# A transformer block on one core: attention scores issued two units ahead, values in pairs, FFN tiles in pools of their own, reloaded operands stored split

## The chip, the cores and the metric

One core of a Trainium2 chip runs one program. The metric is the device time of one execution in microseconds (us). The engines are TensorE (PE, with its weight load PEld), VectorE (DVE), ScalarE (ACT), GpSimd (POOL) and SyncE (SP), which only issues DMAs. Each engine takes its instructions in the order of the program and waits on semaphores; DMAs run on 16 shared DMA engines. PSUM is TensorE's output memory, SBUF the memory of all engines.

## The reference

```
h = modulate(rmsnorm(x), mod0, mod1);  z = h @ w_in        # x: 2048 tokens x 1024
att = neighbourhood_attention(q, k, v, k_ctx, v_ctx, rpb)  # 8 heads of 64, 8x16 query blocks
    s = concat(q.k_loc / 8 + bias, q.k_ctx / 8);  p = softmax(s);  out = p @ concat(v_loc, v_ctx)
y = concat(att, spatial_gating(z), conformer_conv(z)) @ w_out
x = x + mod2 * y
h2 = modulate(rmsnorm(x), mod3, mod4)
gate, up = split(h2 @ w_up)                                # 1024 -> 2 x 2816
x = x + mod5 * ((silu(dwconv(gate)) * up) @ w_down)        # a 3-wide convolution over tokens
return rmsnorm(x)
```

## The kernel before

Everything is fp32. A fp32 operand of a matmul is split into a high and a low part (`hh`, `hl`; for weights the two halves of a `...hl` tile): ACT copies the high part, DVE or POOL subtracts it from the source to get the low one (`halves`, `split_comb`; L1086 and L1087 for weights and for `ah`, L1116 and L1117 for the operands of the FFN). A product of two such operands is three matmuls of 128x512 (high by high, low by high, high by low).

**Attention (318 to 970 us in the trace).** 128 units, each one head of one block of 128 queries: (band, pr, cb, j), where `cb` is one of 4 column blocks and `j` one of a pair of heads. A unit is `scores` (TensorE into the one PSUM bank `s`, then DVE L684 adds the bias into `sb` and takes the maximum `mx`, a small DVE instruction negates it, ACT L689 takes the exponential), `turned` (TensorE transposes `sb` into the PSUM tile `tp`, ACT L719 and DVE L721 copy it to `pt`), and once for each pair of units `values` (TensorE multiplies `pt` by `vt` and `vcx` into `obank`). The order on TensorE is written out: scores(u+1), values(u-2) when `j` is 0, filler, turned(u), filler. The filler is the rest of the projections and of out_proj, pieces of generators; a piece ends at a `yield` with its price.

**The FFN** is a Strassen-Winograd scheme of 7 products over 2x2 blocks, named B11, T2, T1, T3, B21, T4, B22 and numbered 0 to 6 in tile names. Tokens are done in two halves, t = 0 and 1. For t = 0 `first_half` (beside the last piece of out_proj) and `first_half_rest` make the 7 operands in SBUF (`hh{p}_0`, `hl{p}_0`). For t = 1 `second_half` makes them while the up products of t = 0 run, and stores them unsplit to DRAM (`td[p]`); `reload` brings each back as four tiles `tc{p}{kk}` and splits them when the tiles of t = 0 come free. The up products (`g_..`, `u_..`, k = 0 to 10) run from 1062 to 1961 us, with weights staged by `up_weights` (sums on POOL, splits on ACT and DVE). Their results go to DRAM as `actd[t][p]`, one 256 KB store per k and product, issued by POOL.

**The last column.** The convolution needs one token from the other half, so `last_column` makes `pc` at the end of t = 1 and ACT issues five DMAs of single columns into `actd[0]` of T2, T1, T3, T4 and B22.

**The down products (1961 to 2430 us)** load `actd` back as `ra{t}{p}{k}` (two k at a time), split it to `ah`, combine and split weights `wd` to `dw{t}{p}{k}hl` and multiply; `add` adds a product from PSUM to the residual `x1r` (DVE L1450). All these loads go through SyncE's queue in the order of the code. `ahead` is a list of loads to be issued two at a time behind each `ra` load.

SBUF is laid out in pools that open and close in the order of a stack. A tile of a new pool waits for the last users of whatever lay at its address.

## Time and profile before

| | |
|---|---|
| median of 3 runs | 2447.9 us (2447.46 to 2448.69) |
| the profiled execution | 2451.56 us, span 2449.8 us |
| mean granted TensorE clock | 0.972 of full speed |
| PE busy | 2298.1 us, 94% of the span |
| DVE, ACT, POOL busy | 76%, 47%, 44% |
| DMA | 413.35 MB, 169 GB/s over the span |

The profiled execution lies 3.7 us above the median. A busy share is a mean over stages with different limits: TensorE is nearly full in most of them, and idles in a few short stretches, where the granted clock falls too. The time is to be read stage by stage.

### The profile page before, as it was taken

The numbers are of one execution on the slowest core, as the hardware profiler recorded it, in microseconds if no ns is written. First come the engines' busy times: TensorE is split into PE (matmuls) and PEld (weight loads), VectorE is DVE, ScalarE is ACT, GpSimd is POOL, SyncE is SP. The second block draws the span as 40 slices with busy tenths as digits, with TensorE's granted clock in tenths as the row PEclk, the third lists the DMA queues.
The fourth block names the chain that finished last, engine by engine and source line by source line (L and its number), as shares of the span: only waits on it lengthen the run. The fifth ranks groups of instructions, "written<-read, shape, count | busy, mean of one in ns | idle before, by whom it ended". The sixth has DMA issues, their size and how long they took to land.

```text
span 2449.8 us, 34599 instructions
## 1 busy us (share of the span) xinstructions
PE 2298.1 (94%) x12452; PEld 1905.2 (78%) x12452; DVE 1851.2 (76%) x2623; ACT 1146.4 (47%) x2020; POOL 1068.2 (44%) x990
## 2 busy tenths in 40 slices
PE   7999989999999999979999999899999979989996
PEld 5889768988877888858877787588888857868875
DVE  4785665556774974697888878787777769999997
ACT  5764643356455446454443434443443434444442
POOL 0265313011011221355656565366565457565743
PEclk9999999999999999989999999999999989999998
DMA  9675676558768788643334443533233492345322
GB/s 356 224 252 172 209 220 190 173 153 257 222 204 267 215 222 259 216 132 102 130 116 149 137 153 110 169 102 108 94 112 104 126 332 85 94 131 192 95 86 82
DMA packets 183403, 413.35 MB, mean 169 GB/s; under 512 B 27200, under 2 KB 76224, under 8 KB 181184
## 3 DMA queue, kind: packets, MB, share of 16 engines
q1 hardware_dynamic: 142768, 314.63, 41.3%
q0 software_dynamic: 27296, 90.20, 10.0%
q10 hardware_dynamic: 13168, 6.32, 1.0%
q8 instruction: 98, 1.61, 0.3%
q14 instruction: 73, 0.60, 0.1%
HBM read 307.49 MB, written 103.58 MB: 168 GB/s over the span
## 4 chain that ended last, share of the span: by engine, by line
PE 52%; DVE 21%; DMA 12%; issue 7%; POOL 4%; ACT 3%; SPq 1%; DVEq 0%; ACTq 0%; POOLq 0%
PE po L194 4%; DVE cv L565 3%; PE pk L194 3%; PE obank L194 3%; PE pv L1439 2%; PE pq L194 2%; PE tp L200 2%; DMA adaf<-in_ada 2%; PE s L194 2%; PE tp L194 2%; DMA kk<-ks 2%; DVE ah L1087 1%; PE pu L1439 1%; DMA xb<-x1d 1%; POOL ah L1087 1%
## 5 line engine op out<-in xcount | busy, mean ns | idle before, releaser
L565 DVE SCALAR_TENSOR_TENSOR cv<-hconv,cst,cv 128x512 f32<-128x512 f32 x240 | 213.6, 930 | 1.6 <-ACT cv L559 1.4
L684 DVE CUSTOM_DVE_ANT_0 sb<-s,bias_t 128x544 f32<-128x544 f32 (+3 forms) x128 | 105.1, 821 | 107.4 <-PE s L194 95.0
L689 ACT ACTIVATE sb<-sb,mx 128x544 f32<-128x544 f32 (+3 forms) x128 | 106.3, 831 | 156.9 <-DVE mx L687 143.0
L1296 DVE SCALAR_TENSOR_TENSOR c<-gb,cst,c 128x512 f32<-128x512 f32 x176 | 173.6, 1010 | 4.3 <-ACT c L1294 4.2
L1086 ACT ACTIVATE ah<-ra 128x512 fp32r<-128x512 f32 x154 | 94.6, 623 | 114.7 <-PE pu L1439 34.1
L1087 POOL TENSOR_TENSOR ah<-ra,ah 128x512 fp32r<-128x512 f32 x62 | 92.7, 1514 | 76.9 <-ACT ah L1086 76.9
L194 PE MATMUL s<-kk,qq 128*128 128x256 f32 (+4 forms) x512 | 103.0, 323 | 16.0 <-DMA kk<-ks 13.3
L194 PEld LDWEIGHTS s<-kk,qq 128*128 128x128 f32 x512 | 89.6, 193 | 35.3 <-issue 19.4
L200 PE MATMUL tp<-cst,sb 128*128 128x128 f32 (+2 forms) x672 | 98.2, 279 | 12.3 <-ACT sb L689 5.7
L200 PEld LDWEIGHTS tp<-cst,sb 128*128 128x128 f32 (+2 forms) x672 | 78.9, 140 | 25.6 <-ACT sb L689 6.1
L1087 DVE TENSOR_TENSOR ah<-ra,ah 128x512 fp32r<-128x512 f32 x92 | 90.1, 983 | 3.8 <-ACT ah L1086 3.8
L719 ACT ACTIVATE pt<-tp 128x384 f32<-128x384 f32 (+2 forms) x128 | 61.7, 482 | 50.5 <-PE tp L200 50.5
L188 POOL DMA_DIRECT2D x1d<-x x30 | 16.5, 551 | 146.2 <-DVE x L852 137.1
L1294 ACT ACTIVATE c<-gb,cst 128x512 f32<-128x512 f32 x88 | 69.1, 809 | 23.7 <-DVE gb L1269 22.5
L955 POOL TENSOR_TENSOR adaf<-adaf,adaf 128x1024 f32<-128x1024 f32 x16 | 41.8, 2615 | 87.9 <-ACT adaf L952 87.8
L721 DVE COPY pt<-tp 128x256 f32<-128x256 f32 (+1 forms) x128 | 57.5, 450 | 29.9 <-PE tp L200 28.5
L1298 ACT ACTIVATE c<-c 128x512 f32<-128x512 f32 x88 | 55.2, 629 | 43.0 <-DVE c L1296 42.9
L952 ACT ACTIVATE adaf<-adaf,silu_c 128x256 f32<-128x256 f32 x128 | 54.5, 497 | 42.2 <-DMA adaf<-in_ada 42.0
L188 POOL DMA_DIRECT2D actd<-c x66 | 36.5, 554 | 75.5 <-DVE c L1306 58.6
L188 POOL DMA_DIRECT2D ks<-k x60 | 33.5, 561 | 74.9 <-ACT k L218 53.2
L194 PE MATMUL obank<-pt,vt 128*64 128x128 f32 (+2 forms) x832 | 62.5, 285 | 2.1 <-ACT pt L719 2.1
L1306 DVE TENSOR_TENSOR c<-c,u 128x512 f32<-128x512 f32 x66 | 59.6, 904 | 0.4
(2408 smaller groups left out, 7970.6 us busy)
## 6 DMA issues: line engine op xcount, KB each, us to landing
ra<-actd SPq DMA_DIRECT2D x70, 512.0 KB
wg<-in_w_up SPq DMA_DIRECT2D x44, 512.0 KB
wu<-in_w_up SPq DMA_DIRECT2D x44, 512.0 KB
actd<-tt POOLq DMA_DIRECT2D x88, 256.0 KB, 2.4
actd<-c POOLq DMA_DIRECT2D x66, 256.0 KB, 2.3
adaf<-in_ada SPq DMA_DIRECT2D x32, 512.0 KB
qq<-qs SPq DMA_DIRECT2D x64, 256.0 KB
adaf<-in_ada SPq DMA_DIRECT2D x8, 1024.0 KB
```

Source lines behind the costliest of these rows:

```text
L188: st_eng[0].dma_start(plain(dst), plain(src))
L194: x = nc.tensor.matmul(*args, **kw)
L200: x = nc.tensor.transpose(*args)
L565: nc.vector.scalar_tensor_tensor(acc[ct], hb[:, ct, k:k + TB], cvw[:, ct, k:k + 1], acc[ct], op0=ALU.mult, op1=ALU.add)
L684: nc.vector.tensor_tensor_reduce(out=sb[:, w], in0=s[:, w], in1=bt[:, w], scale=1.0, scalar=-3.0e38, op0=ALU.add, op1=ALU.max, accum_out=m ...
L689: nc.scalar.activation(sb[:, w], sb[:, w], AF.Exp, bias=mx[:, 1:2], accum_out=rs[:, cb, j:j + 1])
L719: nc.scalar.activation(dst, src, AF.Copy)
L1086: nc.scalar.activation(hl[:, 0, :], src, AF.Copy)
L1087: eng.tensor_tensor(hl[:, 1, :], src, hl[:, 0, :].bitcast(F32), op=ALU.subtract)
L1294: nc.scalar.activation(c, gb[:, i, o:o + TB], AF.Identity, scale=fcw[:, f, 0:1], bias=fcw[:, f, 3:4])
L1296: nc.vector.scalar_tensor_tensor(c, gb[:, i, o + d:o + d + TB], fcw[:, f, d:d + 1], c, op0=ALU.mult, op1=ALU.add)
L1439: nc.tensor.matmul(ps[i], w[:, ww, sl], ah[:, aa, :], start=start and k_ == 0 and m == 0, stop=(k_ == NP - 1 and m == 2), skip_group_check ...
```

## The change

1. Attention: `scores` is issued two units ahead instead of one, `values` does two blocks (`cb`, `cb`+1) at once, four units late instead of two; its result leaves PSUM in one ACT copy and one DVE multiply for both. The scores are negated in the pass that adds the bias, so the small DVE negation (one for each unit) is gone. `sb`, `pt`, `vt` and `mx` have more buffers, and the filler yields twice as often, at half the price.
2. Pools: the tiles of the FFN's seven operands lie in a pool each, so do the two `mix` buffers and `pair`; small tiles move to the const pool; GpSimd's area for DMA descriptors shrinks from the default, 16384 bytes, to 4096.
3. FFN start: the operand T3 is split within `first_half` instead of behind out_proj.
4. Second half: the operands T2, T1, T3 and T4 of t = 1 are split before they are stored (ACT for the high part, DVE for T2 and T1, POOL for T3 and T4), stored as high and low, and `reload` loads them straight into `hh` and `hl`, in two DMAs of 1 MB each.
5. Down: the first three `wd` loads are issued together, all other loads of `ahead` are kept behind the last `ra` load, `x1r` has one pool of 16, the `add` of B11's product is handed out two at a time instead of at once at k = 7, and the low part of B22's `ah` is made by POOL for odd k.

```
-            if x % 2 and x < KT - 1:
-                yield 1.37 * n / TB
+            if x < KT - 1:
+                yield 0.685 * n / TB
...
-        mx = cp.tile([P, 2], F32, tag="mx", name="mx" + nm, bufs=2)
+        sb = pool.tile([P, 768], F32, tag="sb", name="sb" + nm, bufs=3)
+        mx = cp.tile([P, 1], F32, tag="mx", name="mx" + nm, bufs=3)
...
-        x = nc.vector.tensor_scalar(mx[:, 1:2], mx[:, 0:1], -1.0, None, op0=ALU.mult)
+        x = nc.vector.tensor_tensor_reduce(out=sb[:, w], in0=s[:, w], in1=bt[:, w], scale=-1.0,
+                                           scalar=3.0e38, op0=ALU.add, op1=ALU.min, accum_out=mx)
...
-            if u + 1 < len(units):
+            if u + 2 < len(units):
                 with hot():
-                    scores(*units[u + 1], pool)
-            if j == 0 and u:
+                    scores(*units[u + 2], pool)
+            if cb % 2 == 0 and j == 0 and u:
                 with hot():
-                    values(*units[u - 2][0:3], pool)
+                    values(*units[u - 4][0:3], pool)
...
-            for p, x in ((B11, b11), (T2, b22), (T1, b12)):
+            for p, x in ((B11, b11), (T2, b22), (T1, b12), (T3, t3)):
                 split_comb(p, kk, x, nc.gpsimd if p == B11 else nc.vector)
...
             for p in range(7):
-                store(td[p][:, kk, :], cs[p])
+                c = cs[p]
+                if p in SPLIT:
+                    c = halves(c, fws, "sp", 3, f"tbs{kk}{p}", nc.vector if p < 3 else nc.gpsimd)
+                store(td[p][:, kk], c)
...
             new_comb(p, 1)
+            if p in SPLIT:
+                for i in range(2):
+                    load(hcomb[p][i], td[p][:, :, i, :])
+                continue
...
-        wd_load(0, 0, 0)
+        for c in range(3):
+            wd_load(0, 0, c)
...
-                        load(at[:, 0:n, :], actd[t][p][:, k:k + n, :])
+                        last_ra[0] = load(at[:, 0:n, :], actd[t][p][:, k:k + n, :])
                     ah = halves(at[:, k % 2, :], dah, "ahl", 6, f"ah{t}{p}{k}",
-                                nc.gpsimd if p in (B11, B21, T4) and (t or p or k > 3) else nc.vector)
-                    for f_, args in islice(ahead, 2):
-                        f_(*args)
-                    if mid and k == 7:
-                        mid()
+                                nc.gpsimd if p in (B11, B21, T4) and (t or p or k > 3) or p == B22 and k % 2 else nc.vector)
+                    with tc.issue_after(last_ra[0]):
+                        for f_, args in islice(ahead, 2):
+                            f_(*args)
+                    for _ in islice(mid, 2 if k > 2 else 0):
+                        pass
...
-    nc = _bacc.Bacc("TRN2", target_bir_lowering=False, num_devices=1)
+    nc = _bacc.Bacc("TRN2", target_bir_lowering=False, num_devices=1, dynamic_dma_scratch_size=4096)
```

How it moves instructions, at three places. First VectorE at the start of the FFN: `x130` to `x137` are the residual adds that empty the PSUM tiles of the last out_proj, `wg0_0hl0` to `wg0_0hl6` the low parts of the first gate weights. Before:

```order
L302 TENSOR_TENSOR ssum_last_10523<-ssum_last_10523,sqn236_10823 128x512
L1107 SCALAR_TENSOR_TENSOR xe41_10972<-xe41_10972,a2_105,r21_10384 128x512
L852 SCALAR_TENSOR_TENSOR x137_10863<-po_37_10838,modv_103,xr37_10836 128x512
L1087 TENSOR_TENSOR wg0_0hl0_10902<-wg0_00_10246,wg0_0hl0_10902 128x512
L1087 TENSOR_TENSOR wg0_0hl2_10908<-wg0_0s0_10894,wg0_0hl2_10908 128x512
L1107 SCALAR_TENSOR_TENSOR xe51_10978<-xe51_10978,a2_105,r21_10384 128x512
L302 TENSOR_TENSOR ssum_last_10523<-ssum_last_10523,sqn237_10866 128x512
L1087 TENSOR_TENSOR wg0_0hl1_10905<-wg0_0s1_10895,wg0_0hl1_10905 128x512
L1087 TENSOR_TENSOR wg0_0hl3_10911<-wg0_0s2_10896,wg0_0hl3_10911 128x512
L1087 TENSOR_TENSOR wg0_0hl4_10914<-wg0_00_10246,wg0_0hl4_10914 128x512
```

Of the change:

```order
L1097 TENSOR_TENSOR wg0_0hl0_10789<-wg0_00_10128,wg0_0hl0_10789 128x512
L310 TENSOR_TENSOR sqn220_9760<-sqn220_9760,sqn227_10326 128x512
L1097 TENSOR_TENSOR wg0_0hl2_10795<-wg0_0s0_10781,wg0_0hl2_10795 128x512
L1097 TENSOR_TENSOR wg0_0hl1_10792<-wg0_0s1_10782,wg0_0hl1_10792 128x512
L859 SCALAR_TENSOR_TENSOR x130_10386<-po_30_10337,modv_113,xr30_10335 128x512
L1097 TENSOR_TENSOR wg0_0hl3_10798<-wg0_0s2_10783,wg0_0hl3_10798 128x512
L1097 TENSOR_TENSOR wg0_0hl4_10801<-wg0_00_10128,wg0_0hl4_10801 128x512
L1097 TENSOR_TENSOR wg0_0hl5_10804<-wg0_01_10129,wg0_0hl5_10804 128x512
L318 RECIPROCAL n22c_10418<-n22c_10418 128x4
L859 SCALAR_TENSOR_TENSOR x131_10455<-po_31_10399,modv_113,xr31_10397 128x512
```

The splits of the first weights have moved from behind `x137`, the last of those adds, to ahead of `x131`.

Second, SyncE's queue at the reload: `tc{p}{kk}` are the tiles that are split after loading, `hl{p}_1` and `hh{p}_1` the operands themselves, `wu1_..` and `wg1_..` weights. Before:

```order
L185 DMA wu1_00_14671<-in_w_up 128x1024
L185 DMA wu1_01_14672<-in_w_up 128x1024
L185 DMA tc12_14442<-td1_81 128x512
L185 DMA tc13_14446<-td1_81 128x512
L185 DMA wg1_10_14839<-in_w_up 128x1024
L185 DMA wg1_11_14840<-in_w_up 128x1024
L185 DMA tc20_14452<-td2_82 128x512
L185 DMA tc21_14456<-td2_82 128x512
L185 DMA tc22_14460<-td2_82 128x512
L185 DMA tc23_14464<-td2_82 128x512
```

Of the change:

```order
L193 DMA wu1_00_14544<-in_w_up 128x1024
L193 DMA hl1_1_14362<-td1_91 128x4x512
L193 DMA hh1_1_14361<-td1_91 128x4x512
L193 DMA hl2_1_14366<-td2_92 128x4x512
L193 DMA hh2_1_14365<-td2_92 128x4x512
L193 DMA wu1_01_14545<-in_w_up 128x1024
L193 DMA hl3_1_14370<-td3_93 128x4x512
L193 DMA hh3_1_14369<-td3_93 128x4x512
L193 DMA hl5_1_14392<-td5_95 128x4x512
L193 DMA hh5_1_14391<-td5_95 128x4x512
```

The loads of T2, T1, T3 and T4 stand ahead of the weights `wg1_1..`, and are 1 MB each; the ones of T2 stood behind them as quarters before their split.

Third, the same queue at the start of the down products. Before:

```order
L185 DMA wd000_17869<-in_w_down 128x2048
L185 DMA wd004_17870<-in_w_down 128x2048
L185 DMA wd008_17871<-in_w_down 128x1536
L185 DMA x1r000_17875<-x1d_78 128x512
L185 DMA x1r001_17876<-x1d_78 128x512
L185 DMA x1r002_17877<-x1d_78 128x512
L185 DMA x1r003_17878<-x1d_78 128x512
L185 DMA x1r010_17879<-x1d_78 128x512
L185 DMA ra000_17896<-actd00_87 128x1024
L185 DMA ra002_17936<-actd00_87 128x1024
L185 DMA ra004_17974<-actd00_87 128x1024
L185 DMA wd010_17863<-in_w_down 128x2048
```

Of the change:

```order
L193 DMA wd000_17754<-in_w_down 128x2048
L193 DMA wd004_17755<-in_w_down 128x2048
L193 DMA wd008_17756<-in_w_down 128x1536
L193 DMA ra000_17783<-actd00_97 128x1024
L193 DMA ra002_17821<-actd00_97 128x1024
L193 DMA ra004_17859<-actd00_97 128x1024
L193 DMA ra006_17898<-actd00_97 128x1024
L193 DMA wd010_17748<-in_w_down 128x2048
L193 DMA ra008_17938<-actd00_97 128x1024
L193 DMA wd014_17749<-in_w_down 128x2048
L193 DMA wd018_17750<-in_w_down 128x1536
L193 DMA ra0010_17956<-actd00_97 128x512
```

The first `ra` loads stood behind five loads of the residual `x1r`, and stand now right behind the weights.

## Rows read from the trace of the kernel before

**Rows 1.** The page, busy time: engine, us (share of the span), instructions.

```profile
PE 2298.1 (94%) x12452; PEld 1905.2 (78%) x12452; DVE 1851.2 (76%) x2623; ACT 1146.4 (47%) x2020; POOL 1068.2 (44%) x990
```

**Rows 2.** Stretches: length, busy of PE, PEld, DVE, ACT, POOL (instructions), clock, DMA, GB/s.

```profile
318.00:970.00 652.00, 619.39 (x4620) 531.44 (x4619) 418.90 (x922) 334.85 (x638) 114.76 (x117) 0.97 0.72 217
970.00:1062.00 92.00, 88.53 (x443) 72.55 (x442) 63.49 (x74) 41.58 (x65) 34.15 (x29) 0.98 0.60 197
1062.00:1100.00 38.00, 24.61 (x80) 17.99 (x80) 38.00 (x43) 22.27 (x40) 21.15 (x15) 0.78 0.34 112
1100.00:1500.00 400.00, 392.27 (x1714) 321.90 (x1713) 333.61 (x396) 167.18 (x275) 254.12 (x292) 0.99 0.38 129
1500.00:1570.00 70.00, 57.12 (x205) 39.21 (x205) 52.15 (x68) 31.81 (x54) 26.20 (x28) 0.90 0.48 157
1570.00:1960.00 390.00, 389.13 (x1717) 321.64 (x1716) 299.75 (x387) 159.69 (x258) 219.65 (x222) 1.00 0.33 108
1960.00:2030.00 70.00, 52.37 (x214) 41.74 (x213) 47.70 (x45) 25.69 (x46) 39.39 (x32) 0.88 0.86 296
2030.00:2450.00 420.00, 383.59 (x1648) 310.19 (x1646) 386.15 (x389) 173.56 (x303) 242.16 (x153) 0.97 0.36 111
```

**Rows 3.** TensorE in order of time, down products: start, us, line, names, count.

```profile
2176.59 2.88 PE L1439 MATMUL pu<-ah,dw051hl 128*128 128x512 f32 x12
2179.31 2.88 PE L1439 MATMUL pu<-ah,dw052hl 128*128 128x512 f32 x12
```

**Rows 4.** TensorE's waits, 318 to 970 us: total, times, longest.

```profile
PE s L194 <- DMA kk<-ks: 13.3, 7, 5.5
PE tp L200 <- ACT sb L689: 5.7, 2, 3.6
PE tp L200 <- ACT pt L719: 5.3, 2, 3.4
PE s L194 <- DVE mx L684: 2.7, 3, 2.1
```

**Rows 5.** TensorE's waits, 1036 to 1100 us.

```profile
PE g_0x L1250 <- DVE hl L1117: 5.9, 2, 3.5
PE g_0x L1250 <- ACT wg_0hl L1086: 4.2, 1, 4.2
```

**Rows 6.** Waits of SyncE's DMA queue, 1495 to 1575 us.

```profile
SPq L185 <- DVE hl L1117: 31.6, 19, 13.9
SPq L185 <- DVE wg_0hl L1087: 16.3, 2, 13.7
```

**Rows 7.** TensorE's waits, 1955 to 2030 us.

```profile
PE p L1439 <- ACT ah L1086: 11.4, 2, 10.2
PE p L1439 <- DVE dw044hl L1087: 6.0, 1, 6.0
```

**Rows 8.** Waits of SyncE's DMA queue, 1950 to 1980 us.

```profile
SPq L185 <- PE u_10y L1250: 12.7, 1, 12.7
SPq L185 <- DMA actd<-pc: 12.2, 5, 4.4
```

**Rows 9.** VectorE in order of time, 2004 to 2024 us.

```profile
2008.72 13.42 DVE L1087 TENSOR_TENSOR dw044hl<-wd,dw044hl 128x512 fp32r<-128x512 f32 x1
```

**Rows 10.** GpSimd in order of time, 2002 to 2024 us.

```profile
2004.07 7.66 POOL L1087 TENSOR_TENSOR ah<-ra,ah 128x512 fp32r<-128x512 f32 x6 [6.14 <-ACT ah L1086]
```

**Rows 11.** VectorE in order of time, 2148 to 2166 us.

```profile
2157.80 0.68 DVE L1408 TENSOR_TENSOR dw069s<-wd,dw069s 128x512 f32<-128x512 f32 x1
2158.41 1.75 DVE L1406 TENSOR_TENSOR dw0610s<-dw0610s,wd 128x512 f32<-128x512 f32 x1
```

**Rows 12.** Groups by line on GpSimd: busy us, mean ns, idle before.

```profile
L1087 POOL TENSOR_TENSOR ah<-ra,ah 128x512 fp32r<-128x512 f32 x62 | 92.7, 1514 | 76.9 <-ACT ah L1086 76.9
L188 POOL DMA_DIRECT2D actd<-tt x88 | 48.4, 552 | 1.1 <-issue 1.1
```

**Rows 13.** The page, DMA issues: KB each, us to landing.

```profile
actd<-tt POOLq DMA_DIRECT2D x88, 256.0 KB, 2.4
```

More of the change, by code (lines that the diff above doesn't have):

```diff
@@ new lines, in values @@
+        o = o_bank()
+        for x in range(2):
+            cb = c0 + x
+            nch, rp = chunking(band, cb)
+            ck = rp * COLS[cb][1]
+            vt, _, pts = steps[band, pr, cb]
+            po = o[:, x * P:(x + 1) * P]
+            for i in range(nch + 2):
+                for j in range(2):
+                    fs = slice(64 * j, 64 * j + 64)
+                    if i < nch:
+                        mm(po[fs], vt[0:ck, i, fs], pts[j][0:ck, i, :], start=(i == 0), stop=False)
+                    else:
+                        c = i - nch
+                        mm(po[fs], vcx[:, c, fs], pts[j][:, 4 + c, :], start=False, stop=(c == 1))
@@ L783, in attend @@
         other(5.0)
-        with hot():
-            scores(*units[0], pool)
-        other(3.0)
+        for u in range(2):
+            with hot():
+                scores(*units[u], pool)
+            other(2.0)
         for u, (band, pr, cb, j) in enumerate(units):
-            if u + 1 < len(units):
+            if u + 2 < len(units):
                 with hot():
-                    scores(*units[u + 1], pool)
-            if j == 0 and u:
+                    scores(*units[u + 2], pool)
+            if cb % 2 == 0 and j == 0 and u:
                 with hot():
-                    values(*units[u - 2][0:3], pool)
+                    values(*units[u - 4][0:3], pool)
             other(rate(u) * 0.35)
@@ L803, in attend @@
         with hot():
-            values(band, pr, cb, pool)
+            values(band, pr, cb - 1, pool)
     obank = []
@@ L1127, in first_half @@
             rs.append(r)
-        for p in (B11, T2, T1):
-            new_comb(p, 0)
         for kk in range(4):
             b11, b12, b22 = (h2_tile(0, kk, i, l, rs, "xa") for i, l in ((0, 0), (0, 1), (1, 1)))
-            t3 = held[T3, kk] = tt(f"ta{kk}")
+            t3 = tt(f"ta{kk}")
             nc.vector.tensor_tensor(t3, b22, b12, op=ALU.subtract)
@@ L1143, in first_half_rest @@
     def first_half_rest():
-        for p in (T3, B21):
-            for kk in range(4):
-                split_comb(p, kk, held[p, kk], nc.vector)
+        for kk in range(4):
+            split_comb(B21, kk, held[B21, kk], nc.vector)
         for kk in range(4):
@@ L1359, in pool @@
             return down.enter_context(tc.tile_pool(name=name, bufs=1, reuse_waits="tile"))
-        dn, da, dw0, dx0, dwh, dx1, dw1, dah, dw2, dx2 = (pool(f"dn{i}") for i in range(10))
-        dnp = down.enter_context(tc.tile_pool(name="dnp", bufs=4, space=PSUM, reuse_waits="tile"))
+        dn, dx, da, dw0, dpad, dwh, dw1, dah, dw2 = (pool(f"dn{i}") for i in range(9))
+        dpad.tile([P, 2048], F32, name="dpad")
+        dnp = Banks(tc, "dn", (("y", 4), ("x", 4)))
+        down.callback(dnp.close)
         LAST = 3
@@ L1417, in tile_hybrid_block, with product @@
             acc = {}
-            def product(p, ps, start, mid=None):
+            def product(p, ps, start, mid=iter(())):
                 at, ops = None, []
@@ L1479, in tile_hybrid_block @@
             y = banks("y", "p2")
-            product(B21, y, True, lambda x=x: [add(x, i, l) for i, l in ((0, 0), (0, 1), (1, 1), (1, 0))])
+            product(B21, y, True, chain(*(adds(x, i, l) for i, l in ((0, 0), (0, 1), (1, 1), (1, 0)))))
             add(y, 0, 0, True)
```

153 lines of the change are left out of this document (70 added, 83 removed).

## The prediction

> **What bounds the kernel now.** I read the busy times first. TensorE is busy for 2298.1 of 2449.8 us [rows 1], so at most 152 us can be won by filling it, and VectorE, with 1851.2, is the only other engine near its limit. A mean over the kernel says little, so the stretches come next [rows 2]. To turn them into losses I need the pace of TensorE at full clock: two groups of 12 matmuls of 128x512 start 2.72 us apart [rows 3], 0.227 us each (a duration shown is longer, since they overlap). In the FFN every product has that shape, so the loss of a stretch is its length less 0.227 times its matmuls: 19.8 us in 1062 to 1100 (80 matmuls), 10.9 in 1100 to 1500 (1714), 23.5 in 1500 to 1570 (205), 0.2 in 1570 to 1960 (1717), 21.4 in 1960 to 2030 (214), and 46 in 2030 to 2450 (1648, the drain at the end included). The loss holds both the idle time and what the lowered clock costs: 0.78, 0.90 and 0.88 in the three short stretches. The steady product loops lose next to nothing; three transitions of 178 us together lose 65. The attention (318 to 970 us) has other shapes; there I go by TensorE's idle time, 652 less 619.39, or 33 us, and by the clock of 0.97.
>
> Then the waits say who is late at each place. In the attention TensorE waits 13.3 us for the loads of keys, 5.7 for the exponential, 5.3 for `pt`, 2.7 for the maximum [rows 4]. At the FFN's start it waits for the low parts of operands and for the first weights [rows 5], and VectorE is busy for 38.00 of 38 us [rows 2], so its queue is the bound there. At the reload it is SyncE's queue that stands, 31.6 us for `hl` and 16.3 for a weight split, each 13.9 or 13.7 at one time [rows 6]: loads wait for tiles that VectorE's splits must release, and weights and operands behind them in the queue wait too. At the start of the down products TensorE stands 10.2 us for the first `ah`, then 6.0 for `dw044hl` [rows 7], while SyncE's queue is held for 12.7 us by residual loads that wait for the last up product and for 12.2 by the column stores [rows 8].
>
> **The change, part by part.** Gains are negative.
>
> *Attention.* With scores two units ahead the exponential and the maximum are ready a unit earlier: the waits of 5.7 and 2.7 us are addressed, 8.4 of the 27 us in [rows 4]. The loads of keys are issued as before and the copies to `pt` follow the transposes as before; I cost both at nothing, and what hides nothing there now hides nothing later. The clock takes up to 0.03 x 652 = 20 us, of which 8.4/27 go with those waits: 6. The upper bound of the gain is 14. The 128 negations leave VectorE, which is busy for 418.90 of 652 us there, so they free nothing that is waited for. Against the gain: the bank `s` is still single, so scores(u+2) must wait for the pass over scores(u+1), which is covered by the pieces of filler between; and values come as 24 to 26 small matmuls in one go where it was 10 to 14. I take -8, between 0 and -14.
>
> *FFN start.* The low parts of the first weights (6 VectorE instructions) and of T3 (4) leave the stretch in which VectorE is full. At its mean there, 38.00 us over 43 instructions or 0.88, that is -8.8 us. They go into the stretch before (970 to 1062 us); out_proj's matmuls run there beside them and VectorE has room (63.49 of 92 us, and the splits wait for nothing later than their weights), so I cost them at nothing; without that cover they would delay the last residual adds by the same 8.8. With a shorter stall the clock of 0.78 (up to 0.22 x 38 = 8.4 us) comes back in part; I take less than half. Together -12, between -4 and -18.
>
> *Second half.* 16 copies on ACT and 8 subtractions on each of VectorE and GpSimd come into 1100 to 1500 us, and the stores grow by 4 MB. VectorE has 66 us free there, GpSimd 146, ACT 233 [rows 2]. A VectorE subtraction takes 0.68 us alone and 1.75 while GpSimd works [rows 11], a GpSimd one 1.51 [rows 12]: 8 x 1.75 + 8 x 1.07 = 22.6 us on VectorE at most, inside its 66. But the loop waits in places for weight splits, and a few of those get 0.7 to 3.5 us later. I take +2, between -2 and +12.
>
> *Reload.* VectorE loses 16 subtractions and ACT 16 copies, and loads land straight in the operands, so the queue no longer waits for splits of these four products. In exchange the bytes grow from 7 to 11 MB. The stretch moved 157 GB/s x 70 us = 11 MB; with 4 more it needs 214 GB/s, and the stretch 1960 to 2030 shows 296 [rows 2]. T2 of t = 1 is wanted some four products (4 x 12 x 0.227 = 10.9 us) after T2 of t = 0 is free. Its 2 MB take 7.1 us at 296 GB/s and 13.4 at 157, plus a landing that I set at the 2.4 us of a store [rows 13]: on time, or 5 us late. T1, T3 and T4 follow every three products or so (8.2 us), so at 157 each is about 5 late, 20 in all, and nothing of the 23.5 is won; at 296 none is. The 157 came from a queue that stood, so the higher rate is nearer. I take -12, between -19 and +4.
>
> *Down start.* The first `ra` loads stand behind the weights instead of behind five residual loads, and B11's product (`actd00`) needs none of the five column stores. They can be issued as soon as the queue reaches them; it stood for 12.7 and 12.2 us at this place [rows 8], so that comes ahead of the end of the up products. The idle 10.2 us should shrink to 1 or 2 (-8.5), and the clock of 0.88, worth up to 0.12 x 70 = 8.4 us, come back in part. The second stall, `dw044hl`, is not a late load: VectorE held that instruction for 13.42 us [rows 9] while GpSimd ran `ah` after `ah` [rows 10]. GpSimd gets the same `ah` in the same burst, and 11 of the adds still stand in a row on VectorE, so I leave this stall as it is. The adds spread and the x1r pool cost nothing: the same instructions, ahead of a product that is 30 us long. -10, between 0 and -19.
>
> *B22.* 10 low parts go from VectorE (0.68) to GpSimd (1.51). Each may hold up one VectorE instruction by 1.07. VectorE is busy for 386.15 of 420 us, so -6.8 to +3.9; I take 0.
>
> **The Trainium skill on this.** The Trainium skill, page "SBUF — State Buffer", section "SBUF: two separate sides", says that VectorE (with two SBUF inputs) and GpSimd share one pair of ports as an exclusive lock, and that whoever comes second is blocked for the whole of the other's instruction. The trace agrees in kind (1.75 against 0.68 us) and goes past it in size (13.42 us over many GpSimd instructions). By that rule each new GpSimd subtraction would cost VectorE one GpSimd instruction, 18 x 1.51 = 27 us; by the rows it is 18 x 1.07 = 19, and the kernel loses it only where VectorE is the bound.
>
> **Sum.** -8 - 12 + 2 - 12 - 10 + 0 = -40. The profiled execution took 2451.56 us, which gives 2411.6; it lies 3.7 above the median of the runs, so the median of the change should be 2408.
>
> **Rivals.** (a) *GpSimd holds VectorE up.* Bursts of GpSimd work as in [rows 10] now also stand in the second half and in B22; the hold of [rows 9] costs TensorE 6 us [rows 7]. Once per kk in the second half (4) plus B22's +4 gives +28 instead of +2: 2434. For it: the row of 13.42 us; against: in 1100 to 1500 VectorE has 66 us free. (b) *The reload stalls by bytes*: 4 in place of -12, 2424. For it: 157 GB/s; against: the 296. (c) *Attention gains nothing or pays*: later stalls take over (the key loads, 13.3 us), and finer switching costs; +6 in place of -8, 2422. (d) *Slower: GpSimd's DMA issues.* The area for its descriptors is a quarter. Should an issue have to wait until the one before has landed, it takes 2.4 us [rows 13] instead of 0.552 [rows 12], 1.85 more. In 1100 to 1500 us GpSimd issues some 44 + 33 stores of `actd` and 28 of `td`: 105 x 1.85 = 194 us on top of 254.12, 48 over the 400. GpSimd becomes the bound and the result is 2408 + 48 = 2456. It decides from 146/105 = 1.4 us per issue. No row before shows such a wait; the Trainium skill, page "DMA: Bandwidth & Descriptors", section "SWDGE vs HWDGE vs iDMA", only says that these rings lie in a part of SBUF, and no run here shows their size to matter. (e) *The stages shift and nothing is won*: each transition has its next late partner (keys, VectorE, the 6.0 us), so the gains of three places come to under 5 us: 2445.
>
> **Chances.** The forecast (2388 to 2419, all four gains at least in part) 0.58; (a) 0.08, (b) 0.10, (c) 0.08, (d) 0.07, (e) 0.06; 0.03 for something slower that I did not price. Two tenths of a per cent, 4.9 us, is about what can be told from no change. (a), (b) and (c) remain faster, so faster is 0.84, same 0.06, slower 0.10. The range is 2385 to 2438: the bounds of the forecast's larger terms and (a), (b), (c).
>
> **What would show it.** Attention right: the waits of `tp` on `sb` gone, the idle time in 318 to 970 down by 8. FFN start: `g_0x` follows `po` without the 4 us wait, the clock near 1. Reload: SyncE's wait for `hl` gone, and TensorE's waits there on DMAs, if any, below 10 us in all. Down: the first `ah` within 2 us of the last up product. Wrong: waits on GpSimd's issues, `tbs` low parts ahead of weight splits, or a TensorE wait on `hh` or `hl` loads above 5 us each.

## The result, and the profile after

The changed kernel takes 2422.65 us (median of 4 runs, 2419.55 to 2432.09), the kernel before 2447.68 us on the same chips: a ratio of 0.9906 (95% interval 0.9876 to 0.9935). That is 25 us faster, inside the range of 2385 to 2438, and 15 us short of the forecast of 2408. The profiled execution took 2424.5 us, with a span of 2422.6.

The page of the changed kernel, busy time as in [rows 1]:

```profile
PE 2288.3 (94%) x12452; PEld 1901.2 (78%) x12452; DVE 1841.5 (76%) x2477; ACT 1139.1 (47%) x1988; POOL 1097.0 (45%) x1008
```

TensorE has the same 12452 instructions. VectorE has 146 fewer (128 negations, 16 splits of the reload and 10 low parts of B22 are gone, 8 new low parts came) and is busy for only 9.7 us less; GpSimd is busy for 28.8 us more. Where the time went is seen in the stretches, cut at the same places of the program in both traces; the columns are those of [rows 2]. The changed kernel:

```profile
328.90:976.80 647.90, 625.15 (x4743) 538.75 (x4745) 408.08 (x799) 333.06 (x616) 116.87 (x120) 0.98 0.74 218
976.80:1079.00 102.20, 90.92 (x379) 72.76 (x376) 87.02 (x94) 53.32 (x85) 47.53 (x38) 0.92 0.58 197
1079.00:1494.00 415.00, 397.15 (x1707) 324.35 (x1706) 353.34 (x410) 177.69 (x294) 267.92 (x298) 0.98 0.39 134
1494.00:1584.00 90.00, 85.99 (x377) 69.98 (x376) 70.79 (x88) 36.09 (x61) 50.59 (x53) 1.00 0.60 216
1584.00:1936.00 352.00, 351.13 (x1550) 290.43 (x1549) 273.28 (x349) 145.15 (x235) 196.49 (x199) 1.00 0.33 108
1936.00:2008.00 72.00, 63.11 (x273) 51.83 (x272) 47.85 (x54) 28.95 (x52) 45.44 (x33) 0.95 0.89 314
2008.00:2404.00 396.00, 375.18 (x1594) 300.78 (x1593) 374.25 (x364) 168.39 (x294) 251.66 (x158) 0.98 0.35 108
2404.00:2422.60 18.60, 1.56 (x4) 0.31 (x3) 11.80 (x9) 2.04 (x3) 4.60 (x3) 0.61 0.31 113
```

The attention, from the first scores to the last values, went from 660.6 to 647.9 us with the same work; in the kernel before, TensorE is busy for 633.53 us of it, in the changed kernel for 625.15. For the other stretches the loss is worked out as in the prediction, length less 0.227 times matmuls, with the kernel before cut at the matching places:

| stage | before | after | change | forecast |
|---|---|---|---|---|
| attention (length) | 660.6 | 647.9 | -12.7 | -8 (0 to -14) |
| last out_proj and FFN start | 116.9 - 416 x 0.227 = 22.5 | 102.2 - 379 x 0.227 = 16.2 | -6.3 | -12 (-4 to -18) |
| up products t = 0, with the second half | 399 - 1710 x 0.227 = 10.8 | 415 - 1707 x 0.227 = 27.5 | +16.7 | +2 (-2 to +12) |
| reload | 94 - 311 x 0.227 = 23.4 | 90 - 377 x 0.227 = 4.4 | -19.0 | -12 (+4 to -19) |
| down start | 74 - 231 x 0.227 = 21.6 | 72 - 273 x 0.227 = 10.0 | -11.6 | -10 (0 to -19) |
| down products | 395.6 - 1636 x 0.227 = 24.2 | 396 - 1594 x 0.227 = 34.2 | +10.0 | 0 (-6.8 to +3.9) |
| drain | 22.2 | 18.6 | -3.6 | none |

With +1.4 us ahead of the first scores the changes come to -25.1; the two spans differ by 27.2, and the rest is some matmuls that differ in count at the cuts. The three transitions and the attention gave 50 us together. Two stages, which the forecast had at +2 and 0, took 27 back.

For the experiments I use the same loss matmul by matmul, called *excess*: the sum of what each matmul's start to the next one's start takes above the usual pace of its shape in that run. It needs no cuts by count, and stays within 3.5 us of the table. Where a run leaves a stage as the changed kernel has it, its excess repeats: within 1.4 us at the FFN's start, 2.1 in the second half, 3.6 at the reload, 1.1 at the down start and 1.8 in the down products (0.3 without e10); the attention's length repeats within 5.4 us.

### The profile page after: what moved, and what is told of

It reads as the page before. It is cut to its first block, busy times and chain, and to the rows that moved or that the text cites. A ratio compares the mean times of both kernels' runs of the same rounds, so it can differ in the third digit from the quotient of the medians.

```text
span 2422.6 us, 34336 instructions
## 1 busy us (share of the span) xinstructions
PE 2288.3 (94%) x12452; PEld 1901.2 (78%) x12452; DVE 1841.5 (76%) x2477; ACT 1139.1 (47%) x1988; POOL 1097.0 (45%) x1008
## 3 DMA queue, kind: packets, MB, share of 16 engines
q0 software_dynamic: 28320, 94.39, 10.4%
## 4 chain that ended last, share of the span: by engine, by line
PE 55%; DVE 16%; DMA 12%; issue 7%; ACT 5%; POOL 4%; SPq 1%; DVEq 0%; ACTq 0%; POOLq 0%
PE po L202 4%; PE pv L1451 3%; PE pu L1451 2%; PE pk L202 2%; DMA adaf<-in_ada 2%; PE p L1451 2%; PE obank L202 2%; PE pq L202 2%; PE tp L202 2%; PE s L202 2%; PE tp L208 2%; DMA bias_t<-in_bias 2%; DVE cv L573 1%; DMA kk<-ks 1%; DMA xb<-x1d 1%
## 5 line engine op out<-in xcount | busy, mean ns | idle before, releaser
L1309 DVE SCALAR_TENSOR_TENSOR c<-gb,cst,c 128x512 f32<-128x512 f32 x176 | 166.1, 968 | 3.1 <-ACT c L1307 2.8
L1097 POOL TENSOR_TENSOR ah<-ra,ah 128x512 fp32r<-128x512 f32 x72 | 112.0, 1569 | 69.4 <-ACT ah L1096 69.4
L1097 DVE TENSOR_TENSOR ah<-ra,ah 128x512 fp32r<-128x512 f32 x82 | 84.3, 1030 | 19.0 <-ACT ah L1096 19.0
L728 DVE COPY pt<-tp 128x256 f32<-128x256 f32 (+1 forms) x128 | 57.7, 450 | 24.5 <-PE tp L208 24.2
L196 POOL DMA_DIRECT2D x1d<-x x30 | 16.6, 553 | 117.3 <-DVE x L859 89.3
L196 POOL DMA_DIRECT2D mixd<-att x14 | 7.7, 550 | 134.2 <-DVE att L227 130.3
```

The source lines that it names most:

```text
L196: st_eng[0].dma_start(plain(dst), plain(src))
L1097: eng.tensor_tensor(hl[:, 1, :], src, hl[:, 0, :].bitcast(F32), op=ALU.subtract)
L1309: nc.vector.scalar_tensor_tensor(c, gb[:, i, o + d:o + d + TB], fcw[:, f, d:d + 1], c, op0=ALU.mult, op1=ALU.add)
```

## The experiments

Each kernel was timed beside the kernel before on its chip, so ratios compare. The intervals of six of the twelve overlap with that of the changed kernel; what tells these apart, and all of them by stage, is the excess in their traces:

```
us of excess          FFN start  second half  reload  down start  down products  attention: length
before                     25.6         13.0    23.0        21.6           24.7              660.6
changed                    19.6         29.1     4.8        10.5           34.0              647.9
e1  lows on VectorE        19.1         18.2     6.7        11.2           34.0              647.1
e2  lows on GpSimd         19.9         21.4     5.0        10.8           34.1              647.1
e3  nothing split          19.4         13.3    24.0        10.9           34.1              645.3
e4  B22 on VectorE         19.5         29.4     3.7        11.2           28.8              648.8
e5  one unit ahead         19.6         28.5     7.0        11.0           34.1              664.8
e6  T3 late                18.3         29.2     4.0        10.4           34.0              650.1
e7  adds at k = 7          18.7         28.9     3.4        10.6           34.1              648.7
e8  columns by SyncE       19.0         29.7     4.2        10.1           34.3              644.7
e9  stores by SyncE        19.2         17.4     5.4        11.2           34.0              646.6
e10 coarse filler          18.8         29.0     5.1        11.5           32.5              658.3
e11 columns in SBUF        19.9         27.6     5.5         0.0           42.2              645.6
e12 three edits            18.5         17.4     4.4         0.0           33.9              647.3
```

### The second half: what holds VectorE up

In the changed kernel TensorE waits four times in the up products of t = 0, 17.3 us together (waits, 1100 to 1500 us):

```profile
PE u_9x L1263 <- ACT u_9p L1272: 5.2, 1, 5.2
PE u_7x L1263 <- ACT u_7p L1272: 4.1, 1, 4.1
PE u_5x L1263 <- ACT u_5p L1272: 4.0, 1, 4.0
PE u_3x L1263 <- ACT u_3p L1272: 4.0, 1, 4.0
```

What lies behind the last of them (`u_9x`) stands in three timelines of 1450 to 1470 us, VectorE first, then GpSimd, then ACT:

```profile
1455.41 1.29 DVE L1097 TENSOR_TENSOR tbs<-tb,tbs 128x512 fp32r<-128x512 f32 x2
1456.62 3.97 DVE L1109 TENSOR_TENSOR tb<-xb,tb 128x512 f32<-128x512 f32 x1
1460.52 0.68 DVE L1282 TENSOR_TENSOR gb<-g_9p,g_9y 128x512 f32<-128x512 f32 x1
```

```profile
1456.40 0.54 POOL L196 DMA_DIRECT2D td<-tbs  x1 [2.35 <-DVE tbs L1097]
1456.95 1.29 POOL L1097 TENSOR_TENSOR tbs<-tb,tbs 128x512 fp32r<-128x512 f32 x1
1458.19 0.56 POOL L196 DMA_DIRECT2D td<-tbs  x1
1458.76 1.27 POOL L1249 TENSOR_TENSOR wg_10s<-wg_10s,wg 128x512 f32<-128x512 f32 x1
1462.80 0.10 POOL L1289 MEMSET gb<- 128x2 f32 x1 [2.77 <-ACT c L1307]
```

```profile
1456.33 0.62 ACT L1096 ACTIVATE wu_9hl<-wu 128x512 fp32r<-128x512 f32 x1
1461.23 1.52 ACT L1307 ACTIVATE c<-gb,cst 128x512 f32<-128x512 f32 x2 [4.28 <-DVE gb L1282]
1462.65 0.57 ACT L1272 ACTIVATE u_9p<-u_9x 128x512 f32<-128x512 f32 x1
```

The subtraction `tb` at 1456.62 takes 3.97 us where its neighbours take 0.68: it ends when GpSimd's run of a store, a low part `tbs`, a store and a weight sum (1456.40 to 1460.03) is over. Behind it VectorE is late with `gb`, ACT stands 4.28 us for `gb` with the copy of `u_9x` behind that, and TensorE waits for the bank that this copy empties. I call this a hold: a VectorE instruction that stands far beyond its usual time beside GpSimd's work. The same happens at all four waits (3.97 to 3.98 us).

Holds of this size are not new in this stretch. The kernel before has five above 3 us between 1100 and 1500 us, and none of TensorE's waits stands behind one of them; one, with GpSimd beside it (1419 to 1424 us):

```profile
1419.21 4.23 DVE L1087 TENSOR_TENSOR wg_9hl<-wg,wg_9hl 128x512 fp32r<-128x512 f32 x1
```

```profile
1418.67 1.08 POOL L188 DMA_DIRECT2D actd<-tt  x2
1419.77 1.30 POOL L1238 TENSOR_TENSOR wu_8s<-wu,wu_8s 128x512 f32<-128x512 f32 x1
1421.01 0.56 POOL L188 DMA_DIRECT2D actd<-tt  x1
1421.58 1.31 POOL L1235 TENSOR_TENSOR wg_9s<-wg 128x512 f32<-128x512 f32 x1
```

The changed kernel has nine there: five, behind which no wait stands either, and the four of `tb`. What is new is the instruction that is held: behind `tb` stands `gb`, and behind that the copy that empties TensorE's bank.

**e1, all low parts on VectorE.**

```
-  c = halves(c, fws, "sp", 3, f"tbs{kk}{p}", nc.vector if p < 3 else nc.gpsimd)
+  c = halves(c, fws, "sp", 3, f"tbs{kk}{p}", nc.vector)
```

> The changed kernel, with all 16 low parts that the second half makes on VectorE (GpSimd loses 8, VectorE gains 8). Theory 'hold': a VectorE instruction with two SBUF inputs stands as long as GpSimd runs without a gap; then the four held tb subtractions fall from 3.98 us to about 2.7, TensorE's waits of u_3x, u_5x, u_7x and u_9x from 17.3 us in all to 8 or less, and the time by 8 to 12 us. Rival 'work': the added instructions delay whichever engine has them; then VectorE, with 8 more, is later, these waits grow to about 22 us and the time by 4.

2416.41 us, ratio 0.9851 (0.9832 to 0.9871). The four held `tb` (L1109) take 0.68 us each, no other `tb` above 1.91, the waits of `u_3x` to `u_9x` fall to 7.7 us, the excess by 10.9. That is 10.9 of the 16 us that the second half costs; the other 5 remain without the holds. The rival "work" is out: VectorE got 8 instructions more and was earlier.

**e2, all on GpSimd.**

```
-  c = halves(c, fws, "sp", 3, f"tbs{kk}{p}", nc.vector if p < 3 else nc.gpsimd)
+  c = halves(c, fws, "sp", 3, f"tbs{kk}{p}", nc.gpsimd)
```

> The changed kernel, with all 16 low parts of the second half on GpSimd. Theory 'hold': GpSimd's runs get longer, the four holds grow to 5 or 6.5 us, TensorE's waits of u_3x to u_9x to about 25 us, the time by 6 to 12. Rival 'work': VectorE is relieved of 8 instructions, the waits fall below 17 us and the time by about 4.

2415.05 us, ratio 0.9847 (0.9829 to 0.9865), excess 21.4: a gain of 7.7 where "hold" expected a loss. So the theory as I had put it, more GpSimd work means longer holds, falls. "Work" had the sign right, but e1 has refuted it. In this kernel GpSimd runs its low parts without stores in between (GpSimd and VectorE, 1445 to 1466 us):

```profile
1450.77 5.04 POOL L1097 TENSOR_TENSOR tbs<-tb,tbs 128x512 fp32r<-128x512 f32 x3 [1.41 <-ACT tbs L1096]
1455.77 1.73 POOL L1249 TENSOR_TENSOR wg_10s<-wg_10s,wg 128x512 f32<-128x512 f32 x1
```

```profile
1452.99 5.05 DVE L1309 SCALAR_TENSOR_TENSOR c<-gb,cst,c 128x512 f32<-128x512 f32 x3
```

Three GpSimd subtractions take 1.68 us each and three VectorE instructions beside them 1.68 each: the two take turns. Nobody is held for this whole run. The changed kernel's run had GpSimd's DMA issues between its tensor instructions, which led to the next experiment.

**e9, the stores issued by SyncE.**

```
-  store(td[p][:, kk], c)
+  nc.sync.dma_start(plain(td[p][:, kk]), plain(c))
```

> The changed kernel with the stores of the second half's operands issued by SyncE instead of GpSimd; who makes the low parts is unchanged. Theory 'issue in the run': the 3.98 us holds of tb need GpSimd's DMA issues between its subtractions; without them the two engines take turns (1.8 us each), TensorE's waits of u_3x to u_9x fall from 17.3 to 4 us or less, the excess of the second half from 29 to about 17, the time by 8 to 12. Rival 'tensor work': the holds stay at 2.6 us or more, the excess at 24 or more. Either way the stores stand in the weights' queue; if that costs, TensorE waits for wu or wg loads.

2410.86 us, ratio 0.985 (0.9831 to 0.9868), excess 17.4, waits of `u_3x` to `u_9x` 9.0 us. The same place (VectorE and GpSimd, 1436 to 1452 us):

```profile
1444.45 0.69 DVE L1109 TENSOR_TENSOR tb<-xb,tb 128x512 f32<-128x512 f32 x1
1445.06 1.78 DVE L1097 TENSOR_TENSOR tbs<-tb,tbs 128x512 fp32r<-128x512 f32 x1
```

```profile
1444.94 1.35 POOL L1097 TENSOR_TENSOR tbs<-tb,tbs 128x512 fp32r<-128x512 f32 x1 [2.95 <-ACT tbs L1096]
1446.25 1.71 POOL L1249 TENSOR_TENSOR wg_10s<-wg_10s,wg 128x512 f32<-128x512 f32 x1
```

`tb` takes 0.69 us and `tbs` on VectorE 1.78, beside the same GpSimd subtraction and sum. All four `tb` take 0.68 to 0.69 us. This agrees with the theory, with the waits at 9.0 us where 4 or less were expected, but it doesn't prove it, because e9 changes two things at once. The issues are out of GpSimd's run; and the run, which started behind VectorE's `tbs` (1456.40) and so together with `tb`, now starts behind ACT's (1444.94), when `tb` has begun. Which of the two ends the holds was not separated. The traces point to the moment at which VectorE's instruction begins: of its 128x512 tensor_tensor and scalar_tensor_tensor instructions from 1100 us to the end of the up products, those above 3 us (9 in the kernel before, 15 in the changed one, 10 in e9) all begin within a GpSimd DMA issue or 0.03 us beside one; of 102 in the changed kernel that take 1 to 3 us and begin within a GpSimd tensor instruction, none is held longer. That is a count, no run moves this alone, and the hold of [rows 9] doesn't fit it: it begins within an `ah`, with no DMA issue in the whole run.

New in this stretch are waits of 1.7 and 1.0 us for splits of `wg` and of 2.0 for a load of `hh`; whether the stores in the weights' queue cause them is not known.

**e3, nothing stored split.**

```
-  SPLIT = (1, 2, 3, 5)
+  SPLIT = ()
```

> The changed kernel with no operand stored split: the second half stores all seven unsplit, the reload splits all seven. Theory 'split' (the gain at the reload, excess 23.0 to 4.8 us, comes from loading split operands): the excess at the reload returns to about 20, that of the second half falls from 29 to about 13, the time stays within 4 us. Rival 'pools' (it comes from tiles in pools of their own, which come free earlier): the excess at the reload stays below 9, and the time falls by about 14 us.

2429.72 us, ratio 0.9909 (0.9893 to 0.9924). Reload 24.0 and second half 13.3, as in the kernel before. The pools alone win nothing at the reload; with the pools in place, loading split operands wins all of it, 19.2 us, and making them costs 15.8 in the second half. Split loads without the pools were not run. As it was written, the edit won 3.4 us net.

### The attention

**e5, scores one unit ahead.**

```
-  if u + 2 < len(units): ... scores(*units[u + 2], pool)
+  if u + 1 < len(units): ... scores(*units[u + 1], pool)
```

> The changed kernel with the scores issued one unit ahead again; values in pairs, buffers, negation and the finer filler stay. Theory 'lookahead' (it gave the 12.7 us that the attention won): TensorE waits for the exponential again (tp on sb, 5 to 8 us), the stretch from the first scores to the last values goes from 648 to 657 to 661 us, the time up by 8 to 13. Rival 'values and filler' (late values and finer pieces gave it): the stretch stays within 3 us of 648.

The loop's start goes with it: one unit of scores stands ahead of it instead of two. 2443.9 us, ratio 0.9974 (0.9957 to 0.9992). The stretch takes 664.8 us, 16.9 more than with two units and 4.2 more than before the change. The profiled execution is the slowest of twelve (2452.17 us), but the ratios say the same: 0.0068 above the changed kernel is 16.6 us. Waits, 318 to 1000 us:

```profile
PE s L202 <- DMA kk<-ks: 22.3, 12, 6.3
PE tp L208 <- ACT sb L696: 8.4, 6, 2.5
```

The waits for the exponential are back, as expected, and those for the keys are at 22.3 us, against 8.4 in the changed kernel and 13.3 in [rows 4]. The changed kernel's 8.4 are two waits, at the first two units. The lookahead hides the key loads too.

**e10, the filler in pieces of the old size,** two units of lookahead kept. Eight `yield`s like this one:

```
-  if x < KT - 1:
-      yield 0.685 * n / TB
+  if x % 2 and x < KT - 1:
+      yield 1.37 * n / TB
```

> The changed kernel with the filler of the attention in pieces of the old size (6 matmuls, old prices). Theory: the finer pieces are part of the attention's gain; then the stretch from the first scores to the last values grows from 648 by 3 to 8 us. Rival: the lookahead alone decides; within 2 us, and the time the same.

2436.82 us, ratio 0.9955 (0.9939 to 0.9971), the stretch 658.3 us, 10.4 more. Waits, 318 to 1000 us:

```profile
PE s L202 <- DVE mx L693: 14.9, 8, 6.7
PE tp L208 <- DVE pt L728: 9.6, 8, 3.0
PE tp L208 <- ACT pt L726: 7.2, 5, 3.1
```

With coarse pieces TensorE reaches the next scores before VectorE has emptied the one bank `s`, for 14.9 us, and the transposes before `pt`. Each of the two edits without the other, beside the rest of the change, gains little against the kernel before or loses (-2.3 and +4.2 us in the stretch); together they gain 12.7.

### The FFN's start

The changed kernel's waits there (1020 to 1100 us), and the VectorE instructions ahead of them:

```profile
PE po L202 <- DVE x L859: 7.4, 2, 4.2
PE u_0x L1263 <- ACT wu_0hl L1096: 2.4, 1, 2.4
```

```profile
1027.21 2.83 DVE L1127 TENSOR_TENSOR hl<-xa,hh 128x512 fp32r<-128x512 f32 x1
...
1030.56 0.74 DVE L859 SCALAR_TENSOR_TENSOR x<-po,modv,xr 128x512 f32<-128x512 f32 x1
...
1043.81 4.37 DVE L1117 SCALAR_TENSOR_TENSOR xa<-xa,a,r 128x512 f32<-128x512 f32 x1
...
1049.31 0.74 DVE L859 SCALAR_TENSOR_TENSOR x<-po,modv,xr 128x512 f32<-128x512 f32 x1
```

The wait for the first weights [rows 5] is gone. In its place `po` waits for `x`, the residual adds that empty the out_proj's banks (1030.56 and 1049.31), behind two held instructions of 2.83 and 4.37 us.

**e6, T3 split late again.**

```
...
-  for p, x in ((B11, b11), (T2, b22), (T1, b12), (T3, t3)):      # first_half
+  for p, x in ((B11, b11), (T2, b22), (T1, b12)):
...
-      split_comb(B21, kk, held[B21, kk], nc.vector)               # first_half_rest
+  for p in (T3, B21):
+      for kk in range(4):
+          split_comb(p, kk, held[p, kk], nc.vector)
```

> The changed kernel with the operand T3 split behind out_proj again, as before. Theory 'VectorE's queue': 4 subtractions of 0.88 us come back into the full stretch, the excess at the FFN's start goes from 19.6 to about 23 us, the time up by 3 to 5. Rival: only the place of the first weights matters there; then within 1.5 us.

2421.36 us, ratio 0.9888 (0.9863 to 0.9913), excess 18.3: no loss. T3's place is worth nothing in this kernel.

### The down start and the down products

The changed kernel, TensorE (1935 to 1956 us) and ACT with its DMA queue (1928 to 1950 us):

```profile
1947.48 4.41 PE L1451 MATMUL p<-ah,dw000hl 128*128 128x512 f32 x12 [8.89 <-ACT dw000hl L1096]
```

```profile
1931.61 14.62 ACTq L1342 DMA_DIRECT2D actd<-pc  x4
1946.28 0.63 ACT L1096 ACTIVATE ah<-ra 128x512 fp32r<-128x512 f32 x1 [14.71 <-DMA wd<-in_w_down]
1946.81 0.61 ACT L1096 ACTIVATE dw000hl<-wd 128x512 fp32r<-128x512 f32 x1
```

TensorE still stands 8.89 us. ACT stands 14.62 us in the issue of four column stores, and the first `ah` and `dw000hl` wait behind them in its order. In the kernel before it stood there too, for 8.66 us (1953.86 to 1962.52), but the first `ah` then waited for its `ra` load until 1970.32, so that these stores did not end TensorE's wait.

**e8, the column stores issued by SyncE.**

```
-  nc.scalar.dma_start(actd[0][p][:, :, TB - 1:], v.unsqueeze(2))
+  nc.sync.dma_start(actd[0][p][:, :, TB - 1:], v.unsqueeze(2))
```

> The changed kernel with the five column stores issued by SyncE instead of ACT. Theory 'ACT's queue': the 8.9 us that TensorE still waits at the down start are ACT's, which stands 14.7 us in the issue of four column stores behind the weight loads before it can copy ah000 and dw000hl; then the wait falls to 1 to 4 us, the time by 5 to 9. Rival 'loads': wd and ra land no earlier; the wait stays at 7 us or more and is then for a DMA.

2425.08 us, ratio 0.9891 (0.9865 to 0.9916). The first down matmul comes right behind the last up product (0.3 us instead of 9.3), but the excess of the stage is 10.1, as before: SyncE now stands 9.73 us in four column stores, `ra` loads come late and TensorE waits 3.1 us for an `ah`, 3.1 for `dw0010hl`, and in smaller pieces. Neither theory said this; the stall followed the stores.

**e11, no column stores.** The columns go from `pc` into the loaded tiles.

```
-  nc.scalar.dma_start(actd[0][p][:, :, TB - 1:], v.unsqueeze(2))        # 5 times
...
+  if t == 0 and p in (T4, B22, T1, T2, T3):                             # behind each ra load
+      c = (T4, B22, T1, T2, T3).index(p)
+      nc.scalar.activation(at[:, 0:n, TB - 1:], pc[:, c, k:k + n].unsqueeze(2), AF.Copy)
```

> The changed kernel without the five column stores: the columns go straight from pc into the loaded ra tiles, by 30 small copies on ACT. Theory 'column stores': they hold whichever queue has to wait for them (SyncE's in the kernel before, ACT's in the changed one, SyncE's again when it issues them); without them the 8.9 us wait falls to 2 us or less and no new wait replaces it, the excess at the down start goes from 10.5 to 4 or less, the time by 6 to 9. Rival 'loads': the loads' bytes are the limit there; the excess stays at 9 or more.

2417.06 us, ratio 0.9881 (0.9862 to 0.99). Stretches of this kernel, the down start and what follows:

```profile
1931.00:1994.00 63.00, 63.00 (x279) 52.16 (x279) 52.55 (x52) 26.68 (x49) 45.79 (x36) 1.00 0.90 345
1994.00:2397.00 403.00, 375.73 (x1587) 301.57 (x1585) 371.01 (x364) 168.86 (x319) 246.03 (x157) 0.97 0.35 106
```

The down start loses nothing: 279 matmuls in 63.0 us, at 345 GB/s, so the loads were not the limit. But the products behind it lose 403 - 1587 x 0.227 = 42.8 us, 8.2 more in excess than the changed kernel. TensorE comes earlier to work that VectorE (busy for 371.01 of 403 us) has not prepared, and waits for it there (waits, 1993 to 2180 us):

```profile
PE fms L1478 <- DVE sq L1473: 4.6, 1, 4.6
PE pv L1452 <- DVE dw069hl L1097: 2.3, 1, 2.3
PE pu L1452 <- DVE dw019hl L1097: 1.6, 1, 1.6
```

The expectation that no new wait would replace the old one was wrong: of the 10.5 us won at the down start, 2.3 are kept. That VectorE is what takes them back is read from these waits; the 30 copies that e11 adds on ACT are a rival that no run takes apart.

**e4, B22's low parts on VectorE again.**

```
-  nc.gpsimd if p in (B11, B21, T4) and (t or p or k > 3) or p == B22 and k % 2 else nc.vector
+  nc.gpsimd if p in (B11, B21, T4) and (t or p or k > 3) else nc.vector
```

> The changed kernel with the low parts of B22's ah all on VectorE again. Theory 'hold': each of the 10 moved subtractions holds VectorE up by 1.10 us and spares it 0.60, so undoing it saves about 5 us: the excess in the down products falls from 34 to about 29. Rival: the larger excess there (34 against 25 before) comes from the adds that are handed out two at a time; then undoing this changes nothing within 2 us.

2420.6 us, ratio 0.9878 (0.986 to 0.9895), excess 28.8, 5.2 less, as expected. A low part on GpSimd costs VectorE more in turns than it saves.

**e7, the adds at once.**

```
-  for _ in islice(mid, 2 if k > 2 else 0):
+  for _ in islice(mid, 16 if k == 7 else 0):
```

> The changed kernel with all 16 adds of B11's product handed out at once at k = 7, as before. Theory: the hold of 13.42 us on dw044hl came from GpSimd's burst meeting VectorE behind the row of adds; then it is back, TensorE waits 4 to 6 us there, the excess at the down start goes from 10.5 to about 16. Rival 'spread is the loss': the adds that are spread lengthen the down products (34 against 25 us of excess, of which B22 is 5); then that falls by about 4 and the down start stays at 10.5.

2425.43 us, ratio 0.9894 (0.9871 to 0.9917). Neither stage moves (10.6 and 34.1). Both theories fall: the 13.42 us hold does not come back with the old adds, and the spread is not what lengthens the down products. The traces show what else differs. In the kernel before GpSimd makes six `ah` in a row from 2004.07 [rows 10], after 6.14 us of waiting, and eight more tensor instructions follow without a gap until 2021.59; in the changed kernel its `ah` at this place come between 1961.23 and 1988.80, at most three in a row (1973.41, 4.25 us), with stores and waits between them. VectorE's adds still come 11 in a row in both (1976.43 in the changed kernel, 1975.91 in e7). That the earlier `ra` loads broke up the burst, and with it the hold, fits these rows; no run tests it.

**e12, three edits together:** e9, e4 and e11.

> The changed kernel with three edits of the earlier runs together: stores of the second half's operands by SyncE, the low parts of B22's ah on VectorE, the columns put into the loaded tiles without column stores. Theory: the first two act in different stages and add up (11.7 and 5.2 us of excess); the third wins 9 us at the down start and gives most back in the products behind it, because VectorE is the bound there, and with B22's burden off it keeps a few of them. Sum -11.7 - 5.2 - 1 to -5: 18 to 22 us below the changed kernel, about 2402. Rival: the down products are bound by VectorE in t = 0 whatever is done, so the third gives nothing and B22 less; then 12 to 15 us below, about 2409.

2398.81 us, ratio 0.9805 (0.9785 to 0.9825): faster than the changed kernel, whose interval is 0.9876 to 0.9935, and 50 us below the kernel before. The second half has 17.4 of excess, the down start none, the down products 33.9, 8.3 less than in e11, where B22's low parts alone were worth 5.2. In the stages that they touch the three edits give 22.3 us together, and 11.7 + 5.2 + 2.3 = 19.2 by themselves: they add up, and a little more.

## Why the prediction was right, and where not

**Right: the direction, the range and the reload; at the down start the number was luck.** The reload gave -19.0 (-12 forecast, at the end of its bounds). In the kernel before TensorE waits 9.2 us there for splits of `hh` and `hl`, the longest of them (1500 to 1575 us):

```profile
PE g_0z L1250 <- ACT hh L1116: 5.2, 2, 3.4
```

In the changed kernel its waits shrink to a DMA's and a copy's (1490 to 1584 us):

```profile
PE g_0y L1263 <- DMA hh<-td: 3.2, 2, 2.6
PE u_10x L1263 <- ACT u_10p L1272: 0.8, 1, 0.8
```

SyncE's queue still stands for `hl` (17.4 us instead of the 31.6 in [rows 6]) and longer for weight splits, and that costs nothing now. Bytes were no limit: the stretch moved 216 GB/s, at the 214 that the prediction asked for. Rival (b) is out. The down start gave -11.6 for -10, but not by the mechanism of the forecast. The wait of 10.2 us, which should have shrunk to 1 or 2, became 8.9. The step "they can be issued as soon as the queue reaches them" was right for the loads (1931.04, ahead of the end of the up products) and overlooked the copies behind ACT's column stores, which held ACT before as well (8.66 us) and hold it for 14.62 now. The 6.0 us wait, which I left as it was, is gone, and the clock of the stage rose from 0.88 to 0.95. "GpSimd gets the same `ah` in the same burst" was wrong: the burst is broken up. e7 shows that the spread adds did not do it; what ended the hold stays open.

**Attention, -12.7 for -8: right in the place, not in the terms.** TensorE's idle time was to fall by 8; it fell by 4.3 (27.1 to 22.8 us). The wait of `tp` for the exponential is gone, the one for the maximum rose from 2.7 to 6.0. The other 8.4 us are busy time, for which the forecast had only 6 us by the clock; over the stretch the clock went only from 0.973 to 0.976. e10 has as little busy time as the changed kernel (623.40 us), so the pieces of the filler are not its source; what the lookahead, the values in pairs and the buffers have in it no run takes apart. The waits for keys, costed at nothing, are part of the gain: e5 has 22.3 us of them, the changed kernel 8.4. And the finer pieces, which I priced only as a risk in rival (c), are needed for it (e10). (c) itself is out.

**FFN start, -6.3 for -12: mis-sized.** The four subtractions of T3, priced at 3.5 us, are worth nothing (e6). The clock of the whole stage went only from 0.91 to 0.92, so little of its share of the 12 came. And what "they go into the stretch before, so I cost them at nothing" left out is seen in the rows: `po` waits 7.4 us for residual adds that VectorE reaches late. That the weight splits ahead of them make them late is argued from the order; the two holds beside GpSimd are in the rows.

**The step that failed: "I take +2" for the second half; it cost 16.7.** The mechanism was named, as rival (a), and its price per place (6 us at four places and +4 for B22) is high for the one, 24 against 16.7 (of which e1 and e9 show 11 to 12 to go with the holds), and near for the other, 5.2. I gave it 0.08 because VectorE had 66 us free in the stretch; the five holds of the kernel before there are not in the forecast. That is the error: free time of an engine says nothing about one instruction that is held while ACT and TensorE stand in order behind it. By the Trainium skill, page "SBUF — State Buffer", section "SBUF: two separate sides", the loser is blocked for the whole of the other's instruction. The turns of e2, e9 and [rows 11] agree with that (VectorE 1.68 to 1.78 us, GpSimd about 1.7); a hold of 3.97 us over two GpSimd tensor instructions and two DMA issues goes beyond it, and there the rows decide.

**The other: "I take 0" for B22 and the down products; they cost 10.0.** 5.2 of it is B22 (e4), where the bound of +3.9 was too low: a VectorE instruction alone makes the next one start 0.61 us later [rows 11], not 0.68, and each turn adds 1.10. The other 4.8 are not taken apart by a run of their own; e7 rules out the spread adds. e11 shows a loss that could be of the same kind: 10.5 us less at the down start come back as 8.2 in the products behind. A start that is 11.6 us better would be paid back in part in the same way; that is argued, not shown.

**Rivals (d) and (e) are out.** The three transitions gave 36.9 us, not under 5. And GpSimd's DMA issue of `actd` takes 552 ns on the mean, as in [rows 12], with the smaller descriptor area:

```profile
L196 POOL DMA_DIRECT2D actd<-tt x88 | 48.4, 552 | 0.0
```

## What to carry to other kernels

When work goes to an engine with free time, look at which single instruction of which other engine it will meet there, and at what stands in order behind that one: four holds, each 3.3 us longer than the instruction alone, cost about 11 us in a stretch where VectorE had 66 us free, while five others in that stretch cost nothing that shows. A stall that is removed ahead of a stretch with another bound can be paid back inside it (8.2 of 10.5 us here), so price it together with that stretch. The column stores held whichever queue issued them; moving them to another queue moved the stall, and only doing without them removed it.

## What was not expected of the hardware

VectorE and GpSimd meet in two ways. They take turns, at about 1.7 us for each instruction of either (e2, e9 and the down products, 1.78 instead of 0.68 on VectorE), or VectorE stands over several of GpSimd's instructions: 3.97 us over a run of 3.6, 4.37 over another, 13.42 in [rows 9]. In the up products of three traces each of the 34 holds above 3 us begins at a GpSimd DMA issue, and taking such issues out of the run at `tb` ended the holds there (e9); but the longest hold begins within a tensor instruction and has no issue in its run, so this is not the whole condition. The column stores, five times 1408 elements of 4 bytes, kept ACT's queue for 14.62 us (four issues) and SyncE's for 9.73 (e8), and ACT's for 8.66 in the kernel before; why the same four issues take so different times is not known.
